# The T5 bias table's background job, cut into a load, a pass, a lookup and a store that run at staggered places

## The chip, the cores and the metric

The kernel runs on one core of a Trainium2 chip. The metric is the device time of one execution in microseconds, taken as the median of three runs. TensorE (PE in the profile) has two clock levels, 1.2 and 2.4 GHz; the profile gives the share of full speed that was granted.

## The reference, cut to what matters

Two transformer-like layers and a third block are computed over 256 rows of 2048 columns. Most of the arithmetic is rows times weights. The change touches one small table that the sparse attention of both layers adds to its logits, the T5 relative position bias:

```python
def t5_bucket(rel):
    rel = jnp.maximum(rel, 0)
    relf = jnp.maximum(rel, 1).astype(jnp.float32)
    large = MAX_EXACT + (jnp.log(relf / MAX_EXACT) / math.log(MAX_DISTANCE / MAX_EXACT)
                         * (N_BUCKETS - MAX_EXACT)).astype(jnp.int32)
    large = jnp.minimum(large, N_BUCKETS - 1)
    return jnp.where(rel < MAX_EXACT, rel, large)
# in sparse_attention:
bias = rel_bias[t5_bucket(pb[:, :, None] - ps)]          # (query, key, head)
logits = jnp.einsum('bqhd,bqkd->bqhk', qb, ks) * scale + bias
```

`rel_bias` has 32 buckets and 8 heads. The kernel computes the table once, for all pairs of a query and a key that can matter: a 128 x 128 part for the first 128 queries (t = 0) and a 128 x 256 part for the others (t = 1), for 8 heads each.

## The kernel before, in words

**Weight chunks.** Every product runs through `wgroup`, which goes over a group of 512 output columns in chunks of two 128-row blocks of the weight. For each chunk `wchunk` loads 512 KB into a tile `raw` (SP issues it, L226; three buffers), ScalarE (ACT) rounds it to `whi` (L231), VectorE (DVE) makes the remainder `wlo` (L233), and TensorE does 12 matmuls with both (L249 to L251). The `raw` buffer is free again when `wlo` is made.

**Background jobs.** After each chunk `wgroup` calls `step()`, which advances a list of Python generators by their rates. A job's piece between two `yield`s is thus issued between two chunks. The T5 job has the rate 0.75 per chunk; at the same time the modulation job streams another weight through DVE (`graw`, loaded at L347, used at L353) at 0.902 per chunk. `until(name)` calls `step()` without chunks until a job has got that far.

**Order on the engines.** Each engine works its queue in order. The framework orders a queue by the place of issue in the program, moved by offsets (`wdma`, `whi`, `wlo` go 20 to 35 places forward), and may put a ready instruction ahead of one that is not. All loads and stores of this stretch go through SP's one queue: weights, modulation weights, T5 blocks and T5 results.

**The stage.** In layer 0 the first ten column groups run over a quarter of the rows of the weight at a time, in four rounds of 20 chunks, as the modulation of the four quarters gets ready. The T5 job is spawned at the start of the second round (about 100 us) and has to be done in the fourth, after the third group (`until("select")`, L856). The table is read only later, by `attend` (L675).

**The T5 job.** `rel_rotary` writes the clipped distances as bytes to `reld` in DRAM (L418). `bias_table` then does 12 blocks of 1024 distances for each of four groups of 32 partitions. For a block it loads `rb` (L457, 128 KB, two buffers). For each half block, three ACT passes (L462, L463, L465) turn distances into a one-hot tile `ohr`, one row for each bucket; a `yield` follows; then two matmuls (L469) look up the 8 heads into PSUM, ACT copies the 32 rows to `bt` (L471), and SP stores them in `biasd` (L472). A third `yield` ends the block. So a block takes three steps, which at 0.75 per chunk is four weight chunks.

Of the kernel before, what the change touches and what calls it, by code (L numbers as in the profile page):

```python
# [7 lines left out]
F32 = mybir.dt.float32  # L8
# [3 lines left out]
U8 = mybir.dt.uint8  # L12
# [6 lines left out]
P = 128  # L19
S = 256  # L20
D = 2048
NH = 8
# [4 lines left out]
LN2 = math.log(2.0)  # L27
# steps of each background job per weight chunk
RATE = {"rows": 0.902, "t5": 0.75, "sel0": 1.421, "sel1": 1.069, "gate0": 0.95, "row1": 0.419, "gate1": 0.42,
        "chain0": 1.0, "chain1": 1.33, "ret0": 1.65, "ret1": 1.254, "late": 0.662, "forget": 0.385,  # L30
        "hgrn": 0.66}
# places that instructions move forward in the order of issue
AHEAD = {"wdma": 20, "whi": 30, "wlo": 35, "gdma": 0, "gdve": -10, "tail": -5}
# [6 lines left out]
def shape_constants():  # L40
    """Tables that depend on shapes alone."""
    f = np.float32
    i = np.arange(P)
    ident = np.eye(P, dtype=f)
    tri = np.where(i[None, :] <= i[:, None], 0.0, NEG).astype(f)
    inv = (f(10000.0) ** (-np.arange(64, dtype=f) / f(64))).astype(f)
    edge = list(range(16)) + [math.ceil(16 * 8 ** (k / 16) - 1e-9) for k in range(16)] + [200]
    lo = np.array([edge[b] for b in i % 32], f)
    hi = np.array([edge[b + 1] - 1 for b in i % 32], f)
    lo, hi = -(lo + hi) / 2, (lo - hi) / 2  # L50
    ones = np.ones((P, P), f)
    blob = np.concatenate([ident, tri, np.broadcast_to(inv, (P, 64)), lo[:, None], hi[:, None], ones], 1)
    lg = np.log1p(-np.exp2(-5.0 - np.arange(NH))).astype(np.float64)
    diff = np.arange(S)[None, :] - i[:, None]
    dec = np.where(diff >= 0, np.exp(lg[:, None, None] * np.maximum(diff, 0)), 0.0) * SCALE
    dec = np.concatenate([dec, dec[:, :, :P]], 2)
    lev = np.zeros((P, 7, P), np.int32)
    for n in range(7):
        L = 1 << n
        lev[:, n, :] = ((i[:, None] // (2 * L) == i[None, :] // (2 * L))  # L60
                        & ((i[:, None] // L) % 2 == 0) & ((i[None, :] // L) % 2 == 1))
    return {
        "k_blob": np.ascontiguousarray(blob, dtype=f),
        "k_dec": np.ascontiguousarray(dec.transpose(1, 0, 2), dtype=f),
        "k_lev": np.ascontiguousarray(lev.reshape(P, 7 * P)),
    }


def build(tc, a, out):
# [4 lines left out]
    with es:  # L74
# [4 lines left out]

        # ---------------------------------------------------------------- helpers  # L80
        def mmt():
# [19 lines left out]
        def step(n=1):  # L101
            """Advance every background job by its rate."""
            for job in list(bg):
# [11 lines left out]
        def spawn(gen, rate, then=None):  # L115
            """Start a background job; another may follow it."""
            bg.append([gen, rate, 0.0, then])
# [10 lines left out]
        def give(consumer, t, pt):  # L128
            """Run a consumer up to its yield; what follows waits for flush()."""
            r = consumer(t, pt)  # L130
            if r is not None:
                next(r)
                late.append(r)
# [15 lines left out]
        def rstd(ss, n, mean):  # L149
            """(ss * mean + EPS) ** -0.5 for a [P, n] tile of sums of squares."""  # L150
            v = sm(n, "rv")
# [16 lines left out]
        def split_ps(ps, gain=None):  # L168
            """A [P, 512] transposed block in PSUM into its two float32r parts."""
            h, l = at_tiles()  # L170
# [35 lines left out]
        def build_kg(src, kg, gains, shifts):  # L206
            """One tile of four transposed blocks: normed rows scaled, shifted, split."""
            ps = transpose4(src)
# [8 lines left out]
        def build_raw(src, kg, gains):  # L217
            """Four transposed blocks of rows that are still to be normed, times the norm's gains."""
            return split_ps(transpose4(src), gains[:, kg * 4:kg * 4 + 4])

        def wchunk(srcs, n, kt):
            """Two row blocks of a weight, loaded and split."""
            raw = wp.tile([P, 2, n], F32, name="raw", tag="raw", bufs=RAW)
# [12 lines left out]
        def wgroup(srcs, n, aT, kts, consumer, mode="k", tw=3):  # L236
            """out[t] = rows[t] @ W for one group of columns; kts are row blocks (pairs from even)."""
            pts = [mmt(), mmt()]
# [39 lines left out]

        # ---------------------------------------------------------------- constants, small vectors
        ct = con.tile([P, 16], F32, name="ct")  # L280
# [44 lines left out]

        # ---------------------------------------------------------------- modulation
        wm = [a["w_mod"][l].rearrange("(p j) n -> p j n", j=16) for l in range(2)]
# [48 lines left out]
        def mod_gate(l, q):  # L376
            """Half q of layer l's gate, on every partition."""
            for acc in gemv(l, [4096 + 1024 * q, 4096 + 1024 * q + 512]):
# [14 lines left out]

        # ---------------------------------------------------------------- T5 bias table, rotary tables
        biasd = [dr.tile([NH, P, (t + 1) * P], F32, name=f"biasd{t}") for t in range(2)]
# [43 lines left out]
        def bias_table(ap):  # L439
# [12 lines left out]
            jobs = [(0, r) for r in range(0, 32, 8)] + [(1, r) for r in range(0, 32, 4)]  # L452
            for t, r0 in jobs:
                ns = (t + 1) * P
                nr = 1024 // ns
                rb = ap.tile([P, nr, ns], U8, name="rb", tag="rb", bufs=2)
                Y.dma_start(rb, bass.AP(tensor=reld[t].tensor, offset=reld[t].offset + r0 * ns,  # L457
                                        ap=[[32 * ns, 4], [0, 32], [1, nr * ns]]))
                h2 = nr // 2
                for hf in range(2):  # L460
# [3 lines left out]
                    ohr = ap.tile([P, 512], F32R, name="ohr", tag="qT", bufs=8)  # L464
                    A.activation(ohr, oh, AF.Relu, bias=ones[:, 0:1], scale=-1.0)  # L465
                    yield
                    pm = mst()
                    for n, pb in enumerate(parts):
                        T.matmul(pm[0:32, :], pb, ohr, start=n == 0, stop=n == 1)  # L469
                    bt = ap.tile([P, 512], F32, name="bt", tag="L", bufs=3)  # L470
                    A.copy(bt[0:32], pm[0:32, :])  # L471
                    Y.dma_start(bass.AP(tensor=biasd[t].tensor,  # L472
                                        offset=biasd[t].offset + (r0 + hf * h2) * ns,
                                        ap=[[32 * ns, 4], [P * ns, NH], [1, 512]]), bt[0:32])
                yield

        # ---------------------------------------------------------------- start
        def square_sum(acc, src):
# [73 lines left out]

        # ---------------------------------------------------------------- block 1
        def from_ps(pt, sb):
            """Columns in SBUF: as they are, or copied out of PSUM."""
            if sb:
# [5 lines left out]
        def layer(l, hT, ap):  # L562
# [62 lines left out]
            def select(t):  # L625
                """0 where a key is among the TOPK of its row and not after it, NEG elsewhere."""
                ns = (t + 1) * P
# [177 lines left out]
            def rot_ret(g, raw):  # L805
                """Rotate and transpose the held columns of half g, then its retention."""
                for n in "qk":
# [18 lines left out]

            # the first ten groups run over parts of the rows, as the modulation of those rows is ready
            groups = [(col(2304), 512, c_qi(0)), (col(2816), 512, c_qi(1)), (ksrc, 336, c_k),
# [45 lines left out]
        def out_proj(l, yT, nxt):  # L874
            """x + gate * (y @ w_out[l]), and the next operand from its rows."""
            xn = [[None] * 4 for _ in range(2)]
# [65 lines left out]

        # ---------------------------------------------------------------- block 2
        w2 = a["w_in_2"][0]
        yT = [[None] * 4 for _ in range(2)]
        kts = list(range(16))
        with tc.tile_pool(name="b2", bufs=1, reuse_waits="tile") as b2:
            # lower bound of the forget gate: softmax over one layer, less the first, clipped
            lb = b2.tile([P, 8], F32, name="lb")
# [57 lines left out]
            def forget(g):  # L1007
                """log f (into Pc) and k = (1 - lb) sigmoid(-f), features on partitions."""
                f = fT[g]
# [218 lines left out]

        # ------------------------------------------------------------ w_o, ple
        def fl(x):  # L1230
            return x.rearrange("p a b -> p (a b)")

        with tc.tile_pool(name="b3", bufs=1, reuse_waits="tile") as b3:
# [45 lines left out]
            def finish(t, jj):  # L1279
                """Final norm of a block of columns, and its store."""  # L1280
                x3 = x2[t][jj]
# [71 lines left out]
```

## Time and profile before

| | |
|---|---|
| median of three runs | 1963.08 us (1960.91 to 1964.33) |
| the profiled execution, first to last instruction | 1964.1 us |
| PE busy, whole span | 1849.0 us, 94% |
| DVE busy | 1313.3 us, 67% |
| ACT busy | 1044.1 us, 53% |
| DMA, mean over the span | 224 GB/s |
| T5 job: first ACT pass to last store | 118.3 to 285.7 us |

The span of the profiled execution lies 1.0 us above the median of the runs. TensorE's busy time is modelled from overlapping matmuls, so its share says little of how fast chunks go by; the number of weight chunks (casts at L231) in a stretch of time says more.

### The profile page before, as it was taken

Reading aid. Unit: us, or ns where it says so; the run is one execution under the profiler, and the core shown is the slowest. Engines: PE = TensorE matmul, PEld = TensorE weight load, DVE = VectorE, ACT = ScalarE, POOL = GpSimd, SP = SyncE. Lnnn points to the kernel's source line nnn. Section 1 sums busy time; section 2 is a strip of 40 time slices with the busy share of each in tenths; the row PEclk is TensorE's granted clock in tenths of the full one; section 3 lists DMA queues with packets and bytes.
Section 4 is the critical chain, followed back from the end, with each engine's and each line's share of the span. In section 5 each row is a group of like instructions: output and inputs, shape, how many; then the busy total and the mean of one; then the engine's idle time right before and its main releaser. Section 6 shows DMA issues by size and latency. Waiting matters only on the chain.

```text
span 1964.1 us, 24148 instructions
## 1 busy us (share of the span) xinstructions
PE 1849.0 (94%) x8670; PEld 1503.6 (77%) x8670; DVE 1313.3 (67%) x1713; ACT 1044.1 (53%) x1576; POOL 93.0 (5%) x220
## 2 busy tenths in 40 slices
PE   3988899998997999999999999999999999999997
PEld 3866577777776877688878878888888888888786
DVE  6787669998777677976755565656575545455554
ACT  3557484554435455447545675458445444445554
POOL 2000011001101002100000100000000000000100
PEclk9999899999998999999999999999999999999999
DMA  9987777987888898875547765556656666657564
GB/s 316 327 269 251 249 234 224 320 293 235 295 300 264 295 309 282 269 223 157 163 156 239 214 181 174 151 171 183 177 151 191 194 193 193 193 183 222 176 205 146
DMA packets 230921, 440.37 MB, mean 224 GB/s; under 512 B 19728, under 2 KB 32144, under 8 KB 230672
## 3 DMA queue, kind: packets, MB, share of 16 engines
q1 hardware_dynamic: 228880, 436.38, 70.5%
q10 hardware_dynamic: 1440, 2.34, 0.3%
q8 instruction: 68, 1.11, 0.2%
q14 instruction: 53, 0.43, 0.1%
q0 software_dynamic: 480, 0.10, 0.0%
HBM read 430.85 MB, written 7.91 MB: 223 GB/s over the span
## 4 chain that ended last, share of the span: by engine, by line
PE 60%; DMA 15%; DVE 11%; ACT 5%; issue 5%; POOL 3%; SPq 1%; ACTq 0%; DVEq 0%; POOLq 0%
PE mm L250 18%; PE mm L251 18%; PE mm L249 18%; DMA graw<-in_w_mod_dram 8%; DVE wlo L233 5%; DMA raw<-in_w_in_dram 4%; DMA rb<-reld 2%; ACT whi L231 2%; DVE acc L353 2%; PE tr L196 2%; PE tr L1070 1%; POOL ry L154 1%; DVE I L648 1%; POOL rv L152 1%; SPq L226 1%
## 5 line engine op out<-in xcount | busy, mean ns | idle before, releaser
L233 DVE TENSOR_TENSOR wlo<-raw,whi 128x1024 fp32r<-128x1024 f32 (+1 forms) x596 | 721.6, 1213 | 409.5 <-ACT whi L231 407.8
L231 ACT CAST whi<-raw 128x1024 fp32r<-128x1024 f32 (+1 forms) x596 | 621.9, 1045 | 696.7 <-PE mm L251 451.3
L250 PE MATMUL mm<-wlo,ah 128*128 128x512 f32 (+1 forms) x2368 | 935.8, 395 | 23.5 <-DVE wlo L233 23.2
L249 PE MATMUL mm<-whi,ah 128*128 128x512 f32 (+1 forms) x2368 | 934.5, 397 | 11.8 <-ACT ah L187 7.7
L251 PE MATMUL mm<-whi,al 128*128 128x512 f32 (+1 forms) x2368 | 931.0, 393 | 0.7 <-DVE al L188 0.6
L250 PEld LDWEIGHTS mm<-wlo,ah 128*128 128x128 f32 x2368 | 449.0, 190 | 132.2 <-DVE wlo L233 44.6
L249 PEld LDWEIGHTS mm<-whi,ah 128*128 128x128 f32 x2368 | 447.7, 189 | 108.8 <-ACT ah L187 8.4
L251 PEld LDWEIGHTS mm<-whi,al 128*128 128x128 f32 x2368 | 448.5, 189 | 92.1 <-DVE al L188 2.2
L353 DVE SCALAR_TENSOR_TENSOR acc<-graw,ct,acc 128x1024 f32<-128x1024 f32 x174 | 223.0, 1282 | 63.4 <-DMA graw<-in_w_mod_dram 62.8
L851 DVE TENSOR_TENSOR sp<-sp,mm 128x512 f32<-128x512 f32 (+1 forms) x64 | 42.0, 660 | 15.1 <-PE mm L251 15.0
L196 PE MATMUL tr<-blob,ev 128*128 128x128 f32 x192 | 34.2, 277 | 5.2 <-DVE ev L737 4.1
L179 ACT ACTIVATE ev<-tr,vT 128x128 f32<-128x128 f32 x112 | 32.4, 378 | 9.9 <-PE tr L196 9.3
L481 ACT ACTIVATE junk<-xs 128x512 bf16<-128x512 f32 (+1 forms) x42 | 25.6, 610 | 21.5 <-DMA xs<-in_x_dram 9.4
L152 POOL TENSOR_SCALAR rv<-tot 128x1 f32<-128x1 f32 (+1 forms) x9 | 3.7, 413 | 652.9 <-DVE tot L203 639.6
L154 POOL TENSOR_TENSOR ry<-rv,mhalf 128x4 f32<-128x4 f32 (+2 forms) x33 | 34.2, 1036 | 2.8
L196 PEld LDWEIGHTS tr<-blob,ev 128*128 128x128 f32 x192 | 23.6, 140 | 13.5 <-issue 6.0
L196 PE MATMUL tr<-blob,xs 128*128 128x128 f32 x128 | 24.5, 285 | 8.8 <-ACT xs L912 6.3
L462 ACT ACTIVATE oh<-rb,blob 128x512 f32<-128x512 uint8 x24 | 16.2, 715 | 27.0 <-DMA rb<-reld 27.0
L1070 PEld LDWEIGHTS tr<-X 128*128 128x128 f32 x224 | 27.0, 192 | 2.0 <-ACT uT L1119 1.0
L1070 PE MATMUL tr<-X 128*128 128x128 f32 x224 | 27.5, 276 | 0.1
L196 PEld LDWEIGHTS tr<-blob,xs 128*128 128x128 f32 x128 | 16.8, 146 | 13.8 <-ACT xs L912 7.4
L469 PE MATMUL ms<-ohr,rb 128*32 128x512 f32 x48 | 16.0, 428 | 11.2 <-ACT ohr L465 11.1
(275 smaller groups left out, 1183.8 us busy)
## 6 DMA issues: line engine op xcount, KB each, us to landing
raw<-in_w_in_dram SPq DMA_DIRECT2D x416, 512.0 KB
graw<-in_w_mod_dram SPq DMA_DIRECT2D x186, 512.0 KB
raw<-in_w_out_dram SPq DMA_DIRECT2D x64, 512.0 KB
raw<-in_w_o_dram SPq DMA_DIRECT2D x32, 512.0 KB
raw<-in_w_ple_gate_dram SPq DMA_DIRECT2D x32, 512.0 KB
raw<-in_w_a_out_dram SPq DMA_DIRECT2D x16, 512.0 KB
raw<-in_w_b_out_dram SPq DMA_DIRECT2D x16, 512.0 KB
raw<-in_w_in_dram SPq DMA_DIRECT2D x16, 256.0 KB
```

Of the source, the lines that this page charges most:

```text
L154: G.tensor_tensor(y, v, mhalf[:, 0:n], op=OP.pow)
L179: A.activation(e[:, s], ps[:, s], AF.Copy, scale=gain[:, i:i + 1])
L196: T.transpose(ps[:, s], src[:, s], ident)
L231: A.copy(hi, raw)
L233: V.tensor_sub(lo, raw, hi.bitcast(F32))
L249: T.matmul(o, ah, hi[:, j, :], start=first, stop=False)
L250: T.matmul(o, ah, lo[:, j, :], start=False, stop=False)
L251: T.matmul(o, al, hi[:, j, :], start=False, stop=end)
L353: last[0] = V.scalar_tensor_tensor(acc, rf, ct[:, j:j + 1], acc, op0=OP.mult, op1=OP.add)
L481: A.activation(junk[:, :n], src, AF.Square, accum_out=acc)
L851: V.tensor_add(h, h, pt[:, :n])
L1070: T.matmul(ps[:, h * P:(h + 1) * P], X[:, h, s], X[:, h, s], start=True, stop=True)
```

## The change

A block's `rb` is now loaded during the first half of the block before it. The lookup of a half block (two matmuls and the copy) is issued one step after the ACT passes of the next half block, and its store one lookup later. One `yield` is added at the end, where the last two stores and the last lookup are issued. The instructions, their shapes and their number are the same. The rest of the diff deletes comments and docstrings.

```diff
             jobs = [(0, r) for r in range(0, 32, 8)] + [(1, r) for r in range(0, 32, 4)]
-            for t, r0 in jobs:
+
+            def load(t, r0):
                 ns = (t + 1) * P
-                nr = 1024 // ns
-                rb = ap.tile([P, nr, ns], U8, name="rb", tag="rb", bufs=2)
+                rb = ap.tile([P, 1024 // ns, ns], U8, name="rb", tag="rb", bufs=2)
                 Y.dma_start(rb, bass.AP(tensor=reld[t].tensor, offset=reld[t].offset + r0 * ns,
-                                        ap=[[32 * ns, 4], [0, 32], [1, nr * ns]]))
+                                        ap=[[32 * ns, 4], [0, 32], [1, 1024]]))
+                return rb
+
+            def look_up(t, r0, ohr):
+                ns = (t + 1) * P
+                pm = mst()
+                for n, pb in enumerate(parts):
+                    T.matmul(pm[0:32, :], pb, ohr, start=n == 0, stop=n == 1)
+                bt = ap.tile([P, 512], F32, name="bt", tag="L", bufs=3)
+                A.copy(bt[0:32], pm[0:32, :])
+                return lambda: Y.dma_start(bass.AP(tensor=biasd[t].tensor, offset=biasd[t].offset + r0 * ns,
+                                                   ap=[[32 * ns, 4], [P * ns, NH], [1, 512]]), bt[0:32])
+
+            held, store = [], []
+            nxt = load(*jobs[0])
+            for n, (t, r0) in enumerate(jobs):
+                rb = nxt
+                nr = 1024 // ((t + 1) * P)
                 h2 = nr // 2
                 for hf in range(2):
                     oh = ap.tile([P, 512], F32, name="oh", tag="sc", bufs=2)
...
                     A.activation(ohr, oh, AF.Relu, bias=ones[:, 0:1], scale=-1.0)
-                    yield
-                    pm = mst()
-                    for n, pb in enumerate(parts):
-                        T.matmul(pm[0:32, :], pb, ohr, start=n == 0, stop=n == 1)
-                    bt = ap.tile([P, 512], F32, name="bt", tag="L", bufs=3)
-                    A.copy(bt[0:32], pm[0:32, :])
-                    Y.dma_start(bass.AP(tensor=biasd[t].tensor,
-                                        offset=biasd[t].offset + (r0 + hf * h2) * ns,
-                                        ap=[[32 * ns, 4], [P * ns, NH], [1, 512]]), bt[0:32])
+                    held.append((t, r0 + hf * h2, ohr))
+                    if hf == 0 and n + 1 < len(jobs):
+                        nxt = load(*jobs[n + 1])
+                    yield
+                    if len(held) > 1:
+                        if store:
+                            store.pop()()
+                        store.append(look_up(*held.pop(0)))
                 yield
+            store.pop()()
+            look_up(*held.pop(0))()
+            yield
```

## Rows read from the trace of the kernel before

**Rows 1.** Busy time by stretch: PE, PEld, DVE, ACT, POOL, clock, DMA share, GB/s

```profile
61.50:95.00 33.50, 33.50 (x156) 27.66 (x155) 25.76 (x25) 18.87 (x24) 0.00 (x0) 1.00 0.97 341
95.00:127.00 32.00, 29.07 (x130) 22.55 (x129) 29.01 (x50) 20.55 (x36) 2.53 (x2) 1.00 0.84 273
127.00:164.00 37.00, 30.35 (x122) 20.93 (x121) 26.89 (x27) 17.48 (x24) 0.00 (x0) 1.00 0.80 252
164.00:192.00 28.00, 25.50 (x123) 19.74 (x121) 20.71 (x26) 22.36 (x37) 0.00 (x0) 1.00 0.88 271
192.00:250.00 58.00, 46.49 (x179) 33.92 (x180) 37.63 (x41) 31.82 (x46) 0.00 (x0) 0.87 0.71 233
250.00:283.00 33.00, 30.94 (x140) 24.31 (x139) 20.69 (x29) 28.71 (x55) 3.71 (x12) 0.92 0.81 257
```

**Rows 2.** The same stretches, casts of weight chunks alone (L231): ACT busy, count

```profile
61.50:95.00 33.50, 12.64 (x12) 1.00 0.97 341
95.00:127.00 32.00, 9.83 (x10) 1.00 0.84 273
127.00:164.00 37.00, 8.38 (x8) 1.00 0.80 252
164.00:192.00 28.00, 7.77 (x8) 1.00 0.88 271
192.00:250.00 58.00, 14.40 (x14) 0.87 0.71 233
250.00:283.00 33.00, 7.76 (x8) 0.92 0.81 257
```

**Rows 3.** T5 instructions from 127 to 250 us, grouped: busy, mean, idle before

```profile
L469 PE MATMUL ms<-ohr,rb 128*32 128x512 f32 x32 | 11.0, 443 | 11.2 <-ACT ohr L465 11.1
L462 ACT ACTIVATE oh<-rb,blob 128x512 f32<-128x512 uint8 x16 | 10.7, 715 | 24.6 <-DMA rb<-reld 24.6
```

**Rows 4.** The chain that ended last, 127 to 160 us: start, length, what

```profile
127.85 5.48 DMA rb<-reld
...
133.35 1.34 ACT oh L462 x2
134.69 1.23 ACT oh L463 x2
135.92 0.85 ACT ohr L465 x2
...
137.05 1.04 ACT whi L231
...
141.41 9.07 DMA rb<-reld
```

**Rows 5.** SP's queue in order of time, parts of 127 to 250 us

```profile
130.00 2.08 SPq L226 DMA_DIRECT2D raw<-in_w_in_dram  x2
138.58 0.60 SPq L472 DMA_DIRECT2D biasd<-bt  x1
...
141.41 0.56 SPq L457 DMA_DIRECT2D rb<-reld  x1
...
241.15 3.49 SPq L457 DMA_DIRECT2D rb<-reld  x2
248.48 0.62 SPq L472 DMA_DIRECT2D biasd<-bt  x1
```

**Rows 6.** SP's waits from 127 to 250 us: total, times, longest

```profile
SPq L472 <- ACT bt L471: 44.0, 10, 7.9
SPq L226 <- DVE wlo L233: 11.7, 10, 3.6
```

**Rows 7.** ACT in order of time, parts of 164 to 184 us

```profile
165.71 1.34 ACT L462 ACTIVATE oh<-rb,blob 128x512 f32<-128x512 uint8 x2 [0.36 <-DMA rb<-reld]
...
178.34 1.33 ACT L462 ACTIVATE oh<-rb,blob 128x512 f32<-128x512 uint8 x2
179.58 0.71 ACT L463 ACTIVATE oh<-oh,blob 128x512 f32<-128x512 f32 x1
180.27 1.06 ACT L231 CAST whi<-raw 128x1024 fp32r<-128x1024 f32 x1
```

**Rows 8.** DMA from 127 to 250 us: packets and bytes of the stretch

```profile
DMA packets 17166, 30.45 MB, mean 248 GB/s; under 512 B 1522, under 2 KB 3307, under 8 KB 17159
```

## The prediction

> **What bounds the kernel now.** I read three things in this order: how fast weight chunks go by in each stretch, which engine is full there, and what the late ones wait for.
>
> First the pace. The count of casts at L231 divides each stretch into chunks [rows 2]. Before the T5 job works, 12 chunks take 33.5 us, 2.79 us each. From 95 to 127 us, where the second round begins and the T5 job has just started, 10 chunks take 32.0 us, 3.2 each. Then 8 chunks take 37.0 us (4.63 each), 8 take 28.0 (3.5), 14 take 58.0 (4.14) and 8 take 33.0 (4.13).
>
> Second, who is full. At 2.79 us a chunk PE is busy all the time and DMA moves 341 GB/s. From 127 to 164 and from 192 to 250 us nothing is full: PE shows 82% and 80%, DVE 73% and 65%, ACT 47% and 55%, DMA 0.80 and 0.71 [rows 1]. PE's share is flattered by overlapping records, but it is clearly below the first stretch. The granted clock is 0.87 in the second of them, so a part of it ran at 1.2 GHz instead of 2.4, after PE's pauses there. A stage in which no engine is full is held by a chain.
>
> Third, the chain. Followed from 127 to 160 us [rows 4] it is: a block's load lands after 5.48 us, six ACT passes run until 136.8, then the cast of the next weight chunk, and the next block's load is issued at 141.41 and lands 9.07 us later. SP shows why the next load is late [rows 5]: after the weight load at 130.00 it stands until 138.58, when it can issue the first T5 store; the next block's load comes only behind the stores, at 141.41. So each block pays in series: landing, six passes, lookup, copy, stores, next load. Loads at 127.85 and 141.41 are 13.6 us apart, and a block is four chunks. From 127 to 250 us ACT stands 24.6 us in front of L462 for the block's load, PE 11.2 us in front of the lookup [rows 3], and SP 44.0 us in ten waits in front of the stores [rows 6]. ACT works in order, so weight casts that have their data stand behind the passes; SP does too, so weight loads stand behind a store whose copy is not made.
>
> **The change, part by part.**
>
> The block load moves from the head of its own block to the first half of the block before: at 0.75 steps a chunk and three steps a block, some four chunks earlier, at the present pace 14 to 18 us. The landings on the chain are 5.5 and 9.1 us [rows 4], so they are covered, even at 2.8 us a chunk (11 us). The 24.6 us of ACT's wait go, in effect all. The very first block has nothing ahead of it and keeps its wait. If the cover were missing, each block would pay its 3.5 us (24.6 over seven waits) again.
>
> The lookup moves one half block back. Its two matmuls (443 ns each in the records, 32 in the stretch, 11.0 us [rows 3]) remain, but the passes they need are then a step older, so PE's 11.2 us go too. Its copy on ACT (L471) moves behind passes of the next half; ACT's work stays.
>
> The store moves one half block further. Its copy is then a step older (1.3 chunks, some 4 us) when SP comes to it. The longest wait for it was 7.9 us and the mean 4.4 [rows 6], and those contained the landing and the passes that no longer come late. I take SP's wait as mostly gone, and bound the rest at a quarter, 11 us, of which weight loads with two other buffers in flight hide most. Each of the moved DMAs still costs SP its 0.56 to 0.60 us of issue [rows 5].
>
> These three waits are the same time seen from three engines, so they aren't added. The saving is the pace: 22 chunks in the two slow stretches take 95.0 us [rows 2], 4.32 each. What would they take? The nearest row is the stretch between them, from 164 to 192 us: there two blocks had landed, or nearly, when ACT came to them (0.36 us of idle time before the passes at 165.71, none before those at 178.34 [rows 7]), and with the whole T5 work and the third quarter's rows beside it 8 chunks took 3.5 us each. It has two narrower chunks in it, which flatters it, and the rows' work, which does the opposite. The other neighbour, 95 to 127 us, gives 3.2. I take 3.4: 22 x 3.4 = 74.8 us, a saving of 20.2 us.
>
> Bounds of this term. Below: 2.79 us a chunk plus the T5 matmuls at the pace at which others follow each other. Half of the 443 ns, since matmuls overlap, is some 0.22 us; 32 of them over 30 chunks add 0.24, so 3.03 a chunk. DMA says nearly the same: 30.45 MB [rows 8] at 341 GB/s are 89 us for 30 chunks, 2.98 each. At 3.03 the 22 chunks save 28 us, and the 8 between them another 4. Above: the pace stays at 3.9 because SP or ACT still hold chunks up, and the saving is 9 us.
>
> The Trainium skill, "DMA: Bandwidth & Descriptors", Specifications, puts the HBM limit of a core at about 358 GB/s. The 341 GB/s of the first stretch agree. By that figure alone the 30.45 MB would take 85 us, an estimate that would move the best case by 4 us and not the forecast.
>
> From 250 to 283 us ACT is busy 28.71 of 33.0 us [rows 1]. The change takes no pass away, so at most 4.3 us are there, and ACT's order decides; the clock is 0.92 there, which less idle time before might mend. I take 1 us, between 0 and 4.
>
> The added step at the end falls into `until("select")`, which runs steps without chunks, so it costs no chunk. The last lookup has its store right behind it, as every lookup has now: one wait of the kind that SP now has ten times, and it is in the count of none gained. Nothing reads the table for the next tens of microseconds. The `ohr` tiles held longer (two or three of eight buffers) and the `bt` tiles (two of three) fit. Cost nothing.
>
> Sum: 20.2 + 1 = 21.2 us, and 1964.1 - 21.2 = 1942.9 for the profiled execution. The median lies 1.0 us below it: **1942**.
>
> **The rivals.**
>
> *The next bound is farther than I think.* PE or DMA fills up as in the first stretch: 28 us less, or with all of both smaller terms 28 + 4 + 4 = 36: 1935 to 1927, 1931 in the middle. For it: both were full at 2.79 us a chunk. Against: DVE now adds partial sums of every chunk group, which it didn't there; its 85 us of work from 127 to 250 [rows 1] would be 94% busy at 3.03 a chunk.
>
> *The wait moves to SP.* Loads and stores stay in one queue. If copies come late because ACT reaches them behind casts that wait for weights, SP still stands in front of stores, and weight loads behind it come late: a pace of 3.9 and a saving of 5 to 12 us, 1951 to 1958, 1955 in the middle. For it: SP's 44.0 us are larger than ACT's 24.6. Against: SP's waits follow the late block, and the copy is a step older. The Trainium skill, "Perfetto Trace Analysis", DMA Optimizations, advises one issuing engine for inputs and another for outputs; by that rule a change that keeps both on SP would land here. The rows on SP agree that stores hold loads up now.
>
> *Nothing comes of it.* The order of the queues is the framework's. It already issues a ready instruction early: two block loads stand together at 241.15, ahead of stores that go at 248.48 [rows 5]. If the new places of issue change little in SP's order, or a shorter stage is paid back by a worse order elsewhere, the time stays within 4 us of 1963.
>
> *Slower.* The block load needs a buffer that the second half's first pass of an earlier block gives free, and there are two. Put into SP's queue too early it stops the queue, weight loads included, until ACT gets there: the pair at 241.15 took 3.49 us instead of 1.1 [rows 5]. With a load in front of the weights in every block this happens up to 11 times. Against it stand the present waits, 24.6 us on ACT and 44.0 on SP, over some 7.5 blocks: 3.3 and 5.9 us a block. So it decides against the change only when a load stops SP for longer than about 9 us a block. At 1.5 us beyond that, 11 blocks cost 16 us: 1979.
>
> **How the numbers follow.** The forecast's case (savings of 12 to 28 us) gets 0.55, the farther bound 0.10, the wait on SP 0.15, no change 0.11, slower 0.09. A measurement of this kernel can tell about 0.2% (4 us) from no change. The first three cases are faster by more: 0.80. Within: 0.11. Slower: 0.09. The range takes in the bounds of the pace and the wait on SP, and half of the case of no change: 1930 to 1961. Outside remain a part of the farther bound, half of no change, and slower: some 0.18.
>
> **What would show it.** Right: no wait of ACT at L462 beyond the first block; PE's wait in front of L469 under 2 us; SP's waits at the stores under 12 us; about 3.4 us a chunk from 127 us on, and the T5 job's last store at some 265 us instead of 285.7; a granted clock of 1.00 through the stretch; everything later as long as before. Wrong: the waits on ACT gone but as much time in front of the weight casts (the raw load or the copy late); SP standing at block loads; the six passes of a block still packed together in front of a cast that PE needs; or the stage shorter and the select or attention part behind it longer by as much.

## The result, and the profile after

The changed kernel takes 1948.88 us (median, 1946.42 to 1950.84), the kernel before beside it 1962.24 us: a ratio of 0.9931, 95% interval 0.9917 to 0.9945, which is 13.4 us (11 to 16) less. The profiled execution has a span of 1944.6 us, 19.5 less than the one before, and it is the fastest of its kernel. So a comparison of the two traces shows some 6 us more than the medians do. A second measurement of the same changed kernel gave 1944.8 us against 1964.32, ratio 0.9891 (0.9865 to 0.9917).

Where the time went is read as in the prediction, by the starts of the casts of chunks (L231). The second round of 20 chunks begins with chunk 20, the fourth with chunk 60 and ends with chunk 80. Microseconds of the profiled executions, as differences of starts rounded to 0.1:

| chunks | before | after | after, again |
|---|---|---|---|
| start of 30 | 127.9 | 130.9 | 129.8 |
| 30 to 60 | 123.0 | 101.9 | 104.1 |
| 60 to 80 | 73.5 | 77.2 | 74.6 |
| 80 to 240 | 545.2 | 537.3 | 542.5 |
| 240 to the end | 1094.5 | 1097.3 | 1094.7 |

The whole gain, 21 and 19 us, is made in the 30 chunks that stand beside the T5 job; 3 and 2 are lost ahead of them, and about 4 and 1 in the next 20. What follows chunk 80 is the same code in both kernels, and the two executions of the changed kernel differ there by 5.2 us between chunks 80 and 240. I count nothing of that for the change.

The stretches after that answer to those before [rows 1]: chunks 30 to 60, 60 to the job's last pieces, and the rest of the fourth round. Columns: PE, PEld, DVE, ACT, POOL busy (count), granted clock, DMA share, GB/s.

```profile
130.50:232.50 102.00, 96.37 (x427) 72.03 (x426) 84.13 (x93) 73.36 (x110) 0.00 (x0) 1.00 0.89 290
232.50:261.80 29.30, 26.37 (x128) 20.35 (x127) 19.43 (x29) 24.73 (x48) 4.30 (x12) 0.98 0.82 253
261.80:309.60 47.80, 46.98 (x206) 35.27 (x204) 36.96 (x81) 26.86 (x62) 11.28 (x24) 0.87 0.71 233
```

PE's share in the first line is 94%, where it was 80 to 91% [rows 1]; the clock is 1.00 all through; DMA moves 290 GB/s. The last line, with no T5 pass in it any more, has a clock of 0.87. Counted on PE, the gain of the 30 chunks has two parts. From 127 to 250 us PE was busy for 102.3 us and idle for 20.7 [rows 1]; in the first line here it is busy for 96.4 and idle for 5.6, with about as many matmul records (424 and 427). So some 15 us are PE's idle time, and some 6 us are matmuls that run at full clock, where the three stretches before had 0.94 on average.

The waits of ACT and SP between chunks 30 and 60. Of the changed kernel, ACT and then SP (total us, times, longest):

```profile
ACT oh L479 <- DMA rb<-reld: 19.8, 8, 4.0
ACT whi L231 <- DMA raw<-in_w_in_dram: 3.6, 5, 1.0
...
ACT whi L231 <- DVE sp L870: 1.7, 1, 1.7
...
SPq L226 <- DVE wlo L233: 41.8, 23, 3.7
SPq L347 <- DVE acc L353: 8.4, 8, 2.2
```

And two lines of ACT before, in the same 30 chunks, that the prediction didn't read:

```profile
ACT whi L231 <- DMA raw<-in_w_in_dram: 18.0, 7, 5.3
ACT whi L231 <- DVE sp L851: 6.2, 1, 6.2
```

ACT's wait for the T5 block (L479 is the old L462) fell from 24.6 us [rows 3] to 19.8 only. Its wait for weights fell from 18.0 to 3.6, the one for partial sums from 6.2 to 1.7, the one of the copy for the lookup from 2.5 to nothing: 4.8 + 14.4 + 4.5 + 2.5 = 26.2 us, less some 3 us of small new waits. In these 30 chunks ACT's idle time went from 50.4 to 28.6 us, by 21.8, about what they became shorter (21.1). So more than half of the gain on ACT is weights that come in time. SP shows why: it has no wait at a T5 store in these chunks, where it had 51.4 us before: 41.9 put down to the copy L471, as the 44.0 of [rows 6] from 127 to 250 us, and 9.5 put down to other ACT instructions. Instead it stands 41.8 us, 12.5 before, where a weight load waits for a `raw` buffer to come free. It is now ahead of the chunks, not behind them. At the stores it has 12.7 us left from 110 to 285 us, all after chunk 60:

```profile
SPq L468 <- ACT bt L467: 6.3, 2, 3.2
SPq L468 <- ACT oh L479: 3.0, 2, 2.4
SPq L468 <- ACT junk L500: 2.4, 1, 2.4
SPq L468 <- ACT oh L480: 1.0, 1, 1.0
```

### The profile page after: what moved, and what is told of

It reads as the page before. It is cut to its first block, busy times and chain, and to the rows that moved or that the text cites. A ratio compares the mean times of both kernels' runs of the same rounds, so it can differ in the third digit from the quotient of the medians.

```text
span 1944.6 us, 24147 instructions
## 1 busy us (share of the span) xinstructions
PE 1848.2 (95%) x8670; PEld 1505.5 (77%) x8670; DVE 1313.3 (68%) x1713; ACT 1043.4 (54%) x1576; POOL 94.8 (5%) x220
## 4 chain that ended last, share of the span: by engine, by line
PE 65%; DMA 13%; DVE 11%; ACT 4%; issue 4%; POOL 2%; SPq 1%; ACTq 0%; DVEq 0%; POOLq 0%
PE mm L249 20%; PE mm L250 20%; PE mm L251 20%; DMA graw<-in_w_mod_dram 7%; DVE wlo L233 4%; DVE acc L353 3%; DMA raw<-in_w_in_dram 2%; ACT whi L231 2%; PE tr L196 1%; PE tr L1089 1%; DMA raw<-in_w_out_dram 1%; POOL ry L154 1%; DMA rb<-reld 1%; PE ms L656 1%; DMA ev<-xd 1%
## 5 line engine op out<-in xcount | busy, mean ns | idle before, releaser
L231 ACT CAST whi<-raw 128x1024 fp32r<-128x1024 f32 (+1 forms) x596 | 621.2, 1044 | 668.1 <-PE mm L251 463.6
L249 PE MATMUL mm<-whi,ah 128*128 128x512 f32 (+1 forms) x2368 | 934.4, 397 | 12.3 <-ACT ah L187 7.6
L870 DVE TENSOR_TENSOR sp<-sp,mm 128x512 f32<-128x512 f32 (+1 forms) x64 | 41.8, 658 | 9.6 <-PE mm L251 9.4
L500 ACT ACTIVATE junk<-xs 128x512 bf16<-128x512 f32 (+1 forms) x42 | 25.6, 610 | 21.3 <-DMA xs<-in_x_dram 10.3
L479 ACT ACTIVATE oh<-rb,blob 128x512 f32<-128x512 uint8 x24 | 16.3, 716 | 21.6 <-DMA rb<-reld 21.6
L867 ACT COPY sp<-mm 128x512 f32<-128x512 f32 (+1 forms) x32 | 18.0, 566 | 14.3 <-PE mm L251 14.2
```

The costliest lines, as they stand in the source:

```text
L231: A.copy(hi, raw)
L249: T.matmul(o, ah, hi[:, j, :], start=first, stop=False)
L500: A.activation(junk[:, :n], src, AF.Square, accum_out=acc)
L870: V.tensor_add(h, h, pt[:, :n])
```

## The experiments

Two theories stood at the start. By the prediction's (theory A), the block's landing ahead of its passes holds the stage, so that the load issued ahead carries the gain. By the rival (theory B), it is SP's stand in front of the stores, which holds up the weight loads behind them and which the lag of lookup and store takes away. Three more came later: that ACT still waits for blocks because its passes moved up with the load (theory C), that the store's own lag is what frees SP (theory D), and that what T5 still costs after the change is ACT's pass work (theory E). Each median stands beside the kernel before on the same chip, with the ratio and its 95% interval; "30 to 60" and "60 to 80" are times of these chunks in the one profiled execution, "start of 80" is how late chunk 80 begins there, and "SP" is the sum of SP's waits at T5 stores between chunks 30 and 60 (none where GpSimd issues them).

| kernel | median us | ratio | 30 to 60 | 60 to 80 | start of 80 | SP |
|---|---|---|---|---|---|---|
| before | 1962 to 1966 | 1 | 123.0 | 73.5 | 324.4 | 51.4 |
| after | 1948.9 | 0.9931 (0.9917 to 0.9945) | 101.9 | 77.2 | 310.0 | 0 |
| after, again | 1944.8 | 0.9891 (0.9865 to 0.9917) | 104.1 | 74.6 | 308.5 | 0 |
| load ahead only | 1957.4 | 0.9963 (0.9941 to 0.9986) | 114.4 | 71.9 | 316.1 | 25.6 |
| lags only | 1960.4 | 0.9974 (0.9952 to 0.9996) | 112.7 | 81.0 | 321.9 | 13.6 |
| before, stores on GpSimd | 1947.1 | 0.9920 (0.9892 to 0.9947) | 106.3 | 78.3 | 313.5 | none |
| after, passes pinned | 1956.8 | 0.9950 (0.9935 to 0.9965) | 109.7 | 76.7 | 317.6 | 9.0 |
| after, store without lag | 1947.2 | 0.9926 (0.9891 to 0.9960) | 102.2 | 76.0 | 309.1 | 8.7 |
| no T5 work | 1935.4 | 0.9844 (0.9824 to 0.9864) | 97.6 | 71.6 | 297.6 | 0 |
| after, one pass | 1947.3 | 0.9918 (0.9894 to 0.9942) | 104.3 | 73.4 | 307.6 | 1.3 |
| after, compare on GpSimd | 1948.0 | 0.9913 (0.9885 to 0.9942) | 108.3 | 76.0 | 314.0 | 1.6 |
| after, stores on GpSimd | 1950.7 | 0.9914 (0.9891 to 0.9938) | 97.8 | 81.3 | 310.2 | none |
| after, rate 0.85 | 1949.6 | 0.9914 (0.9899 to 0.9929) | 105.2 | 74.7 | 313.8 | 0.3 |
| after, both of these | 1940.7 | 0.9893 (0.9856 to 0.9929) | 99.7 | 71.0 | 303.9 | none |

**The changed kernel again.** The same code, measured beside the first experiments.

> The changed kernel once more, beside the parts of it. Its profiled execution was 19.5 us shorter than that of the kernel before, its median 13.4 us. If the difference is the luck of where TensorE's clock falls, this run shows again 1946 to 1951 us, with the block waits of ScalarE (21.6 us before the first pass) and the T5 stretch at 3.4 us a chunk unchanged, and half-clock stretches in another place or of another length.

1944.8 us (1940.41 to 1947.46), just under what was expected. ACT's wait for blocks was 24.1 us in nine waits and SP's at the stores about 11. So the waits of the trace above are not an accident of one execution; the two medians differ by 4 us.

**One part alone: the load ahead.** The kernel before with nothing but the block load moved; lookup and store as before.

```diff
+            nxt = load(*jobs[0])
...
-                rb = ap.tile([P, nr, ns], U8, name="rb", tag="rb", bufs=2)
-                Y.dma_start(rb, bass.AP(tensor=reld[t].tensor, offset=reld[t].offset + r0 * ns,
-                                        ap=[[32 * ns, 4], [0, 32], [1, nr * ns]]))
+                rb = nxt
...
+                    if hf == 0 and k + 1 < len(jobs):
+                        nxt = load(*jobs[k + 1])
                     yield
```

> Of the change only the block load, one block ahead; lookup and store stand as in the kernel before. Theory A (the gain is that a block's load no longer waits behind the stores of the block before): ratio to before about 0.993, 1948 us, SP's wait at the stores still 30 us or more. Theory B (the gain is the lag of lookup and store, which frees TensorE and SP): 1958 to 1962 us, TensorE's wait before the lookup still about 10 us.

1957.36 us, 7 us less than before, a third to a half of the 13 to 19 us that the whole change gives. SP's waits at the stores (L480 here), 110 to 285 us, its three largest:

```profile
SPq L480 <- ACT bt L479: 27.3, 7, 6.4
SPq L480 <- ACT oh L469: 17.1, 7, 7.4
...
SPq L480 <- ACT ohr L471: 3.9, 2, 3.2
```

With 0.4 us more that is 48.7 us, against 68.7 before in the same stretch. So two thirds of SP's stand stay (half of it between chunks 30 and 60, 25.6 of 51.4), and ACT's wait for the block is still 19.3 us there (24.6 before).

**The other part alone: lookup and store lag, the load stays at the head of its block.** The edit is against the changed kernel.

```diff
-            nxt = load(*jobs[0])
...
-                rb = nxt
+                rb = load(t, r0)
...
-                    if hf == 0 and n + 1 < len(jobs):
-                        nxt = load(*jobs[n + 1])
```

> Of the change only the lag of lookup and store; a block's load stands at the head of its own block again. Theory A: little gain, 1957 to 1962 us, because each block still pays its landing (ScalarE's wait before the first pass 25 to 30 us). Theory B: about 1949 us, since the stores no longer stop SP and the loads behind them; the wait on ScalarE stays at 25 us without costing anything.

1960.35 us, about 4 us less than before. SP's waits at the stores fall to 23.6 us from 110 to 285 us, ACT's wait for the block is 19.2 between chunks 30 and 60, its wait for weights 14.8. By the medians the parts bring 7 and 4 us alone and 13 to 19 together, but the intervals are too wide to say that they don't add. In the 30 chunks they do: 8.6 and 10.3 us alone, 21.1 and 18.9 together. What holds this kernel's median up lies behind them: the next 20 chunks took 81.0 us, 7.5 more than before, with 13.7 us at half clock. So each theory had given its own part most of the gain, and in the stage each part has about half; each leaves SP a share of its stand at the stores.

**SP's stand by itself.** The kernel before, with nothing but the 24 T5 stores issued by GpSimd, which is idle here.

```diff
-                    Y.dma_start(bass.AP(tensor=biasd[t].tensor,
+                    G.dma_start(bass.AP(tensor=biasd[t].tensor,
```

> The kernel before with its 24 table stores issued by GpSimd instead of SP, nothing else moved. If SP's stand in front of the stores is what holds weights and block loads up, this alone gives a gain of 8 to 14 us (1948 to 1954 us) and SP's waits of 71 us in front of the stores are gone. If the chain runs through landing, passes and lookup without SP, the time stays within 4 us of 1962.

1947.09 us, ratio 0.9920: by the medians as fast as the changed kernel, with the old order of load, passes and lookup. This decides between the two theories. Waits between chunks 30 and 60, ACT's and then SP's largest:

```profile
ACT oh L462 <- DMA rb<-reld: 18.4, 6, 5.3
ACT whi L231 <- DMA raw<-in_w_in_dram: 6.2, 5, 1.9
...
SPq L226 <- DVE wlo L233: 43.0, 23, 4.0
```

The wait for the block is nearly as long as in the changed kernel, the wait for weights is down from 18.0 to 6.2, and SP stands at free buffers as there. A queue that isn't blocked by a store brings the gain, and the load ahead isn't needed for it. Whether it brings all of it is less sure: chunk 80 begins at 313.5 us here and at 310.0 and 308.5 in the changed kernel, and the rest of this execution's gain lies behind it, where nothing was counted for the change either. The last column of the table says the same by degrees, in one execution each: with 51 us of SP's waits in the 30 chunks they took 123 us, with 26 and 14 us 114 and 113, with 9 us 110 and 102, with less than 2 us or a queue that has no T5 store 98 to 108. The Trainium skill, "Perfetto Trace Analysis", DMA Optimizations, says that it may make sense to issue inputs on one engine and outputs on another; this run agrees with it (0.9920).

**The wait for the block taken away.** Why didn't it go? In the program the passes of block 2 (blocks and chunks are counted from 0) stand behind chunks 33 and 34. ACT's queue in the changed kernel, in order of time (start, length, line; the idle time before in brackets):

```profile
130.89 1.03 ACT L231 CAST whi<-raw 128x1024 fp32r<-128x1024 f32 x1
...
134.68 1.34 ACT L479 ACTIVATE oh<-rb,blob 128x512 f32<-128x512 uint8 x2 [1.38 <-DMA rb<-reld]
135.92 0.71 ACT L480 ACTIVATE oh<-oh,blob 128x512 f32<-128x512 f32 x1
136.54 1.03 ACT L231 CAST whi<-raw 128x1024 fp32r<-128x1024 f32 x1
```

The first cast is chunk 30, the last chunk 31. Both first passes of the block stand between them, two to three chunks earlier than written, and wait for a load that SP issued at 125.95 and that landed after 8.7 us. In the kernel before, both stood behind the cast of chunk 34 and began at 150.50 us, after 2.36 us of idle time. Given a load that comes some four chunks earlier, the framework's ordering put the passes four chunks earlier too, up to the landing again. That is theory C. This kernel ties the first pass of each half behind the cast of its own chunk:

```diff
-                A.copy(hi, raw)
+                last_cast[0] = A.copy(hi, raw)
...
+                    with tc.issue_after(last_cast[0].ins):
+                        A.activation(oh, rb[:, hf * h2:(hf + 1) * h2, :].rearrange("p a b -> p (a b)"), AF.Abs,
+                                     bias=bmid)
```

> The changed kernel with the first pass of each half block tied behind the cast of the weight chunk that it is issued with, so that ScalarE cannot run it two or three chunks early, as soon as its load is due. Theory C (ScalarE still waits 21 to 24 us for blocks because the passes moved up with the load): the wait falls under 6 us. If that wait costs time, the kernel gets faster than the changed one by 5 to 15 us (about 1935 us); if it is idle time of an engine that nothing needs then, the time stays within 4 us of the changed kernel (1945 to 1949).

1956.82 us, ratio 0.9950: 8 to 12 us slower than the changed kernel by the medians, 4 to 12 by the ratios to the kernel before. Neither of the expected times came (1935, or 1945 to 1949). Its waits, 110 to 285 us (its lines are one to three higher):

```profile
ACT whi L232 <- DMA raw<-in_w_in_dram: 17.2, 14, 3.7
ACT bt L468 <- PE ms L466: 16.7, 6, 5.5
...
PE mm L250 <- ACT whi L232: 8.9, 8, 2.4
...
ACT oh L481 <- DMA rb<-reld: 2.3, 1, 2.3
```

The wait for the block is gone, from 21.6 to 2.3 us in this stretch, as the prediction wanted it; so theory C holds. In its place ACT stands 16.7 us in front of copies of lookups that are now late, and 17.2 instead of 5.3 in front of weights; PE waits more for casts (8.9 instead of 4.7). The total for the block is thus no measure of what it costs: ACT has idle time in this stage, and taken from one place it turns up at another, here at a worse one. What the wait by itself costs isn't shown, since the tie also fixes an order that the kernel didn't have.

**The store without its lag.** Each lookup's store is issued right behind it; load ahead and the lookup's lag stay.

```diff
-                        if store:
-                            store.pop()()
-                        store.append(look_up(*held.pop(0)))
+                        look_up(*held.pop(0))()
...
-            store.pop()()
```

> The changed kernel with each store issued right behind its lookup again; block load and lookup stay where the change put them. Theory D (the stores' place in SP's queue carries the gain, as the run with stores on GpSimd says): SP stands 30 us or more in front of the stores and the time goes back to 1955 us or more. If the earlier load and the later lookup carry it: 1945 to 1950 us, whatever SP's stand is.

1947.15 us, ratio 0.9926, the 30 chunks in 102.2 us: the same as the changed kernel, though SP's waits at the stores are 25.0 us instead of 12.7. So theory D missed. The load ahead and the lookup's lag together carry the change; the half block more for the store adds nothing that can be measured here. It doesn't follow that SP's stand costs nothing: theory D asked for 30 us or more, and of the 25.0 us only 8.7 lie between chunks 30 and 60, where the load ahead alone leaves 25.6.

**What T5 costs in all.** The whole T5 work left out: no loads, passes or lookups; the 24 stores write a constant tile, so the table isn't computed.

> The changed kernel without the T5 job's loads, ScalarE passes and lookups; the 24 stores are kept and write a constant tile (so the table is left out of the computation). It gives the stretch its floor: with TensorE or DMA as the bound 2.8 to 3.1 us a chunk, 88 to 92 us for 30 chunks, and 1930 us or less. If the stretch still takes 100 us, the rest of the hold-up is not the T5 job's.

1935.35 us. The T5 job cost the kernel before 30.5 us, and it still costs the changed one some 11 to 17 (30.5 less the 19.5 and 13.4 of the change); the profiled executions are 11.2 and 12.3 us apart. In the same 30 chunks:

```profile
128.00:225.80 97.80, 86.48 (x385) 67.50 (x385) 84.25 (x94) 35.77 (x42) 0.00 (x0) 1.00 0.87 290
```

ACT now waits almost only for weights (54.8 us), SP for the most part for free `raw` buffers (39.8), and a chunk still takes 3.25 us, more than the expected 2.8 to 3.1. This is the floor of the stage: the changed kernel with 3.40 is 4.3 us above it for the 30 chunks (6.5 in the second trace), and DMA's 290 GB/s are the same in both.

**Is the rest ACT's passes?** Two changes of the changed kernel: one pass instead of three (the second and third are left out), and passes 2 and 3 as one compare on GpSimd. The first doesn't compute the table any more; the second does, and its edit is shown.

```diff
-                    A.activation(oh, oh, AF.Relu, bias=bhw)
-                    A.activation(ohr, oh, AF.Relu, bias=ones[:, 0:1], scale=-1.0)
+                    G.tensor_scalar(ohr, oh, bhw, 0.0, op0=OP.add, op1=OP.is_le)
```

> The changed kernel with one ScalarE pass per half block in place of three (the second and third pass are left out of the computation). About 24 x 2 x 0.62 = 30 us of ScalarE's work go. Theory E (what the T5 job still costs, 11 to 15 us over a kernel without it, is ScalarE's time in front of weight casts): 1935 to 1940 us. If it is the lookup on TensorE or the T5 job's transfers: 1944 to 1950 us.

> The changed kernel with the second and third pass done as one comparison on GpSimd, which is busy 5% of the time; the table is the same. Theory E: 1936 to 1942 us, unless a comparison takes so long (over 3 us) or holds VectorE up so much that it gives that back; then within 4 us of the changed kernel or slower.

1947.32 and 1948.03 us, no faster than the changed kernel. From 130 to 234 us ACT is busy 55.3 and 51.8 us instead of 75.4, and what is saved comes back as waits: for weights 19.1 and 19.0 us between chunks 30 and 60, instead of 3.6. Theory E falls. In the second the compare is also slow, and PE waits 6.6 us for it (chunks 30 to 60):

```profile
L481 POOL TENSOR_SCALAR ohr<-oh,blob 128x512 fp32r<-128x512 f32 x17 | 39.2, 2315 | 71.7 <-ACT oh L479 71.7
```

**SP free and T5 done sooner.** The changed kernel with its stores on GpSimd, with the T5 job's rate at 0.85 a chunk instead of 0.75, and with both.

```diff
-RATE = {"rows": 0.902, "t5": 0.75, "sel0": 1.421, "sel1": 1.069, "gate0": 0.95, "row1": 0.419, "gate1": 0.42,
+RATE = {"rows": 0.902, "t5": 0.85, "sel0": 1.421, "sel1": 1.069, "gate0": 0.95, "row1": 0.419, "gate1": 0.42,
...
-                return lambda: Y.dma_start(bass.AP(tensor=biasd[t].tensor, offset=biasd[t].offset + r0 * ns,
+                return lambda: G.dma_start(bass.AP(tensor=biasd[t].tensor, offset=biasd[t].offset + r0 * ns,
```

> The changed kernel with its table stores issued by GpSimd, so that SP issues weights and block loads alone. If what is left of SP's stand in front of stores (13 us in the changed kernel) still holds weights up, 4 to 8 us less than the changed kernel (about 1939 us). If the lag has already done what a queue of their own does, no more than 3 us apart.

> The changed kernel with the T5 job's rate at 0.85 steps a chunk in place of 0.75, so that its last blocks are done before the third group of the last round, where ScalarE is full and TensorE pauses and falls to 1.2 GHz. If that crowd costs 5 to 7 us: about 1940 us, without the half-clock stretch near 262 us. If the denser passes take it back before: within 4 us of the changed kernel.

> The changed kernel with the stores issued by GpSimd and the T5 job's rate at 0.85. Stores on GpSimd alone gave the T5 stretch its floor (98 us for 30 chunks) but then a half-clock stretch of 13.7 us and 8 us more for the next 20 chunks. If that tail is the T5 job's last blocks meeting the key group's work on ScalarE: the tail falls to 72 to 75 us and the time to about 1940. If the tail comes from the select job itself: 1946 to 1951 us.

1950.7, 1949.55 and 1940.7 us. The stores on GpSimd alone bring the 30 chunks to 97.8 us, the floor, and lose it in the next 20 (81.3 us, with 13.7 us at half clock). The rate alone changes nothing that can be measured: its next 20 chunks take 74.7 us, but chunk 30 begins at 133.9 us, 3 us later than in the changed kernel, as more T5 work now lies ahead of it. With both, chunk 30 begins at 133.2 us, the 30 chunks take 99.7 us and the next 20 take 71.0, the floor of the kernel without T5 (71.6):

```profile
132.80:232.70 99.90, 93.44 (x410) 69.97 (x410) 81.25 (x89) 76.46 (x113) 10.61 (x19) 0.98 0.91 296
232.90:303.90 71.00, 66.53 (x334) 52.16 (x332) 61.56 (x116) 45.94 (x100) 16.17 (x40) 0.98 0.82 268
```

Its median is the lowest of all that compute the table, as expected, but its interval (0.9856 to 0.9929) overlaps those of the changed kernel, whose second measurement (0.9891) it nearly equals. That it beats the changed kernel is suggested (chunk 80 begins 4.6 to 6.1 us earlier in the traces) and not shown. After the change, the separate engine of which the Trainium skill speaks ("Perfetto Trace Analysis", DMA Optimizations) brings nothing measurable by itself (0.9914).

## Why the prediction was right, and where it failed

The direction and the pace were right; 1942 was forecast, 1948.9 came. By its steps:

- **No engine full, a chain holds the stage.** Right: without T5 work the same chunks take 97.6 instead of 123.0 us with a busier DMA (0.87 instead of 0.78). But the reading of the chain was half wrong. It made "landing, six passes, lookup, copy, stores, next load" one series in which each link counts. The run with stores on GpSimd keeps landing, passes and lookup in their old order and by the medians gains as much as the change. What counted was the link from the stores to the weight loads behind them.
- **"The 24.6 us of ACT's wait go, in effect all."** Failed: 19.8 us stay, 22.5 in the second trace. The step put the passes where the program has them, four chunks behind the load; the framework moved them up behind the earlier load. And the wait wasn't worth its length: with it removed by force the kernel got slower.
- **"These three waits are the same time seen from three engines."** Failed in that form. It was the reason not to add them, which was right, but it let me take ACT's wait at the block for the one to remove. The row for the casts' own wait for weights (18.0 us, now 3.6) was left out of the prediction. It is where most of ACT's gain is seen. And SP's 44.0 us were read too low: they are the waits put down to the copy alone, and all of SP's waits at the stores from 127 to 250 us add up to 53.5.
- **PE's 11.2 us before the lookup go, to under 2.** Right: no such wait of PE is left; its weight loads wait 1.6 us there.
- **SP's waits at the stores mostly go, under 12 us.** Right but for 0.7 us: 12.7 (11 in the second trace), and none of it between chunks 30 and 60.
- **The pace.** Right: 22 x 3.4 + 8 x 3.5 = 102.8 us were forecast for the 30 chunks, 101.9 and 104.1 came. In part that was luck: the neighbour was taken because its blocks had landed, which is not what acts. It was also the stretch in which SP stood least at the stores, 9.9 us over 8 chunks, beside 15.0 over 8 and 28.5 over 14 in the two slow stretches, and that the prediction didn't read. The clock, some 6 of the 21 us, is in the pace without a price of its own: the neighbour had 1.00 throughout. The lower bound of 3.03 was too low: the floor without any T5 work is 3.25. These chunks have more beside T5 than those of the first stretch (DVE is busy 86% of the time without T5, 77% from 61 to 95 us [rows 1]), which may be why; that wasn't tested. With it the rival of a farther bound falls: it asked for 28 to 36 us, where T5's whole cost was 30.5.
- **The last store at some 265 us.** Right, 264.0.
- **The tail gains 1 us (0 to 4).** Failed: the 20 chunks from 60 on lost 3.7 us in the one profiled execution and 1.1 in the other. The bound "below" was set at nothing, with the reason that no pass is taken away; but the change can alter which work meets there. T5's last pieces now stand among the key group's copies on ACT, PE pauses for DVE's results, and right behind that the clock is at half. That T5's pieces cause the pauses isn't shown: the kernel without T5 work has the same two waits (0.9 and 1.0 us), with 3.4 us at half clock. Waits of PE from 245 to 280 us, and the stretch that follows:

```profile
PE tr L623 <- DVE ev L619: 1.5, 1, 1.5
PE tr L622 <- DVE wi L614: 1.0, 1, 1.0
...
261.00:274.00 13.00, 12.87 (x36) 9.44 (x37) 7.59 (x12) 7.40 (x21) 0.89 (x2) 0.50 0.70 228
```

  13 us at 0.50, which is 1.2 GHz, in which 36 matmuls keep PE busy; half of it, some 6.5 us, is lost where PE is the bound. The prediction expected the clock at 1.00 through the stretch. It is that through the 30 chunks (but for 3.4 us in the second trace), where the kernel before had four pieces of 3.4 to 6.8 us at half clock between 194 and 256 us, 20.4 in all; 13.7 come back at the job's end.
- **"Everything later as long as before."** Between 240 and the end to 2.8 and 0.2 us; between 80 and 240 it was 7.9 and 2.7 us shorter. All the kernels here take 537 to 549 us for those 160 chunks, in no order that follows the change, so it seems to be the spread of executions. That wasn't tested.
- **A block load that stops SP (the slower case).** It didn't come: SP has no wait at L457 from 110 to 285 us. Its price of 9 us a block had added ACT's wait and SP's, which the prediction elsewhere calls the same time.
- **The rival of the wait moved to SP** (1951 to 1958) is what the load ahead alone gives: 1957, with 48.7 us of SP's waits at the stores. The lags alone gave 1960, outside it.

From the 1944.6 us of the profiled execution back: 1964.1 less 21.1 for the 30 chunks, plus 3.7 for the next 20, plus 3.0 that were lost ahead of chunk 30, less 7.9 and plus 2.8 behind chunk 80. The change's own part, without what follows chunk 80, is 14.4 us by this trace and 15.9 by the second, beside the 13.4 and 19.5 of the medians. The forecast's 21.2 was the gain of the 30 chunks; what it missed is that 2 to 3 us are paid ahead of them and 1 to 4 behind. Its terms for both places were nothing and a gain of 1 us.

What stays open: what makes up the 11 to 17 us that T5 still costs (4.3 to 6.5 of them in the 30 chunks; it isn't ACT's passes), why the stores on GpSimd bring these chunks from 101.9 to 97.8 us when SP had no wait at a store there any more, whether the version with both edits really beats the changed kernel, and why the half-clock stretch behind T5 is 13.7 us in one execution and 6.8 in another of the same kernel.

## What to carry to other kernels

Where loads and stores share one in-order queue, look first at what stands behind the store that waits: a wait of the consumer for the loads behind it (here the casts' 18.0 us) can be worth more than the most visible wait of the job that is being pipelined (24.6 us). Before a wait is costed, ask whether its engine has time to spare and whether the framework's ordering will fill the room again; a single edit that takes away one suspect (the stores on another issuing engine) tells this sooner than the full pipeline. And cost the place where the shortened stage ends: what meets there, and whether TensorE pauses in it.

## What the runs showed of the hardware that was not expected

- One execution differs from another of the same kernel by more than I took: the kernel before ran from 1957.02 to 1971.69 us beside the repeat, the changed one from 1940.41 to 1950.84 over both measurements. Stretches at half clock of 3.4 to 13.7 us lie at other places in nearly every profiled execution (between 100 and 330 us: 20.4 us before, 13.7 and 13.6 after, 3.4 without T5 work).
- Each of the four pieces at half clock before begins in or behind a pause of PE of 1.2 to 4.7 us. Three other pauses of 1.7 to 2.3 us, which end at 137, 154 and 177 us, had none behind them.
- A block of 128 KB took up to 8.7 us from its issue to its landing with DMA 0.89 busy, where 9.07 was one of the longest before [rows 4]. Over the blocks that ACT waited for, it took 5.5 to 9.2 us before and 6.2 to 8.7 after. Issuing it sooner didn't make it shorter.
- A compare of a 128x512 tile on GpSimd took 2.3 us, and ACT's pass over the same tile 0.71.
